# An expert-choice encoder layer on one core: the third expert matrix loaded as pairs of neighbouring rows

## The chip, the core and the metric

The kernel runs on one core of a Trainium2 chip. The metric is the device time of one execution in microseconds (us); the number that counts is the median of the runs shown. TensorE (PE) multiplies matrices, VectorE (DVE) and ScalarE (ACT) work element by element, GpSimd (POOL) does small side work, and SyncE (SP) issues the transfers, which 16 DMA engines carry from device memory (HBM) to the on-chip buffer.

## What is computed

One layer of a hybrid encoder for 512 tokens of 1024 features: three token mixers, an output projection and a norm, and then a mixture of 16 experts of which each picks its 64 best tokens. The change lies in the experts:

```python
def expert_choice_ffn(x, router_w, w_gate, w_up, w_down):
    aff = softmax(einsum('bsd,de->bse', x, router_w))
    gate, idx = top_k(swapaxes(aff, 1, 2), cap)              # cap = 64 tokens an expert
    xs = x[idx]
    h = silu(einsum('becd,edf->becf', xs, w_gate)) * einsum('becd,edf->becf', xs, w_up)
    y = einsum('becf,efd->becd', h, w_down) * gate[..., None]
    # y of all experts is added to the rows of the tokens
```

An expert has three fp32 weights of 8 MB: `w_gate` and `w_up` of 1024 x 2048 (rows of 8 KB) and `w_down` of 2048 x 1024 (rows of 4 KB). 16 experts have 403 MB of them.

## The kernel before

The token mixers, the output projection and the router take the first part of the execution. Then come the experts, one after the other. The weights of expert e are loaded in 24 transfers of 1 MB each, named in the trace e0g, e0u, e0d for its gate, up and down weights (eight loads k = 0 to 7 of each), into tiles of 128 partitions x 2048 floats. `seq` (lines 798 to 811) lists all 384 loads in order, `load_experts` issues them through `load` (line 63) from SP's queue, in that order. A tile is a slot of a shared pool, so a load may start when the tile that had its slot has been read; in the rows of the profile such a wait of SP names the PE work that reads it. The loads run ahead of the arithmetic as far as the slots go. Expert 0's loads are issued while the router still works.

PE takes the loads in the same order. For each gate or up load `ff_mm` (line 1203) multiplies the expert's gathered tokens with it (tiles `pgt` and `pup`). The 2048 hidden features lie as 128 partitions x 1024 columns in `hb`: partitions 0 to 63 hold features 0 to 1023 of the 64 tokens, partitions 64 to 127 hold features 1024 to 2047. ScalarE applies SiLU, VectorE multiplies by the up product (line 1364), then eight transposes on PE (line 1368, tile `pht`) turn `hb` into `hT`, 128 columns at a time. ScalarE copies the first four of them out, VectorE the last four (line 1370). In a transpose the piece of `hb` is the stationary operand (it goes through a weight load, PEld in the profile), and the identity matrix is streamed past it.

`down` (line 1212) multiplies `hT` with the eight down loads (tile `py`). Load k holds, on partition p, row k*128 + p of the weight for the first 1024 features and row 1024 + k*128 + p for the second: two pieces of 4 KB per partition. So load k goes with column block k of `hT`, its first half of slots and its second. The last expert's down weight has a layout and a function of its own (`last_down`). Pairs of experts are gathered together, and the results are added to the rows of the tokens with one-hot products (`pxg`, `pcb`, `pst`), which PE does between the loads of other experts.

Of the kernel before, what the change touches and what calls it, by code (L numbers as in the profile page):

```python
# [7 lines left out]
I32 = mybir.dt.int32  # L8
# [20 lines left out]
def tile_hybrid_layer(ctx, tc, pk, w2p, xT, x, wlv, wa, wak, wmb, wout, eg, eu, ed, out):  # L29
# [45 lines left out]
    # ------------------------------------------------------------ first loads  # L75
# [15 lines left out]
    # the tensor engine's clock and the activation table are up before the first loads arrive  # L91
# [14 lines left out]
    # ------------------------------------------------------------ constants  # L106
# [5 lines left out]
    apT = at_t[:, 0:1536].rearrange("p (b g n) -> p b g n", b=2, g=2)     # transposed probabilities, two buffers  # L112
    dm = at_t[:, 1536:1920]
    masks = at_t[:, 0:384].bitcast(I32).rearrange("p (a b) -> p a b", a=6)    # of the levels, before that
    gD = at_t[:, 384:896].rearrange("p (h b t) -> p h b t", h=2, b=4)         # pairs in 64 tokens
# [16 lines left out]
    # ------------------------------------------------------------ GLA low rank, GLA v, attention v  # L132
    misc = S("misc", [128, 4, 512])          # low rank part, attention v, second key tile's decays
    av = misc[:, 1, :].rearrange("p (a b) -> p a b", a=4)
    # the low rank part is stacked three times on the partitions: high, low, high with high, high, low of its weights
# [8 lines left out]
    def b_mm(pb, k):  # L144
        """products of k-tile k, those first whose parts are there first"""
        for part in range(3):
            for (tb, c), p in pb.items():
                a = (xl if part == 1 else xh)[k // 4][:, k % 4, tb * 128:(tb + 1) * 128]
                w = (wl if part == 2 else wh)[k // 3][:, k % 3, c * 336:(c + 1) * 336]
                PE.matmul(p[:, :336], a, w, start=k == 0 and part == 0, stop=k == 7 and part == 2)  # L150
# [20 lines left out]
    # ------------------------------------------------------------ weight stream of the [feature, token] blocks  # L171
    # block names in order; pairs share a load
    names = ["gq0", "gq1", "gk0", "gk1", "gr0", "gr1", "gr2", "gr3", "ak", "aq0", "aq1", "aq2", "aq3",
             "ch0", "cc0", "cb0", "ch1", "cc1", "cb1", "ch2", "cc2", "cb2", "ch3", "cc3", "cb3"]
    units = []                                   # (kind, chunk, index in chunk)
# [84 lines left out]
    # ------------------------------------------------------------ GLA  # L260
    gqk = S("gqk", [128, 2, 2, 512])             # [q|k, tile, t]
    adec = {}                                    # (direction, tile) -> decay [128, 512]
# [57 lines left out]
    class Gla:  # L320
        """one pass over the two heads of key tile i"""
# [22 lines left out]
        def prep(self, m):  # L344
            """factors of level m (blocks of 2m tokens, decays to the middle)"""
# [59 lines left out]
        def post(self, m):  # L405
            if m >= 256:
                # the rows of k and the state of each half of the tokens
                t = H("gkt" if m == 256 else "gst")
                if m == 256:
                    self.kt = t  # L410
                    A.copy(t, self.p)
                else:
                    self.state = t
                    A.copy(t[:, 0:256], self.p[:, 0:256])
                return
# [70 lines left out]
    def rsqrt(r, h, t):  # L486
        """r = (4.5 h) ** -0.5, as a list of steps: a guess of 1.5 times that from the exponent bits with the sign
        turned, a Newton step that turns it as well and a step of third order that takes the 1.5 away"""
# [9 lines left out]
    def weave(a, b):  # L498
        """the steps of two lists in turn, so that neither waits for its own last step"""
        for i in range(max(len(a), len(b))):  # L500
            run(a[i:i + 1] + b[i:i + 1])
# [5 lines left out]
    # ------------------------------------------------------------ attention  # L507
    aq = [S(f"aq{i}", [128, 4, 512], F32R) for i in range(2)]     # high and low parts
# [10 lines left out]
    class Att:  # L519
        """heads j and j + 4, query block b"""  # L520
# [79 lines left out]
    # ------------------------------------------------------------ short convolution  # L600
# [25 lines left out]
    # ------------------------------------------------------------ side work beside the blocks  # L626
# [3 lines left out]
    class Step:  # L630
        """work beside a segment of the blocks: before it, on the tensor engine after it, and afterwards"""
# [38 lines left out]
    def overlay(a, b, at):  # L670
        """steps b beside steps a from position at of a"""
        for i, o in enumerate(b):
            if at + i < len(a):
                a[at + i].join(o)
            else:
                a.append(o)
        return a
# [79 lines left out]
    # ------------------------------------------------------------ gates, branches, merge  # L757
    order = ("g", "c", "a")
    accs, mh, ml = [], [], []
    # ------------------------------------------------------------ output projection: its weights  # L760
# [36 lines left out]
    # ------------------------------------------------------------ expert weights  # L797
    seq = []
    for e in range(NE):
# [4 lines left out]
        for k in range(8):  # L804
            if e < NE - 1:
                seq.append((ed[e].rearrange("(h q p) d -> q p h d", h=2, p=128)[k], e, "d", k))
            else:
                src = ed[e].rearrange("(f p) d -> p f d", p=128)
                seq.append((src[:, k % 2 * 8:k % 2 * 8 + 8, k // 2 * 256:k // 2 * 256 + 256], e, "d", k))
    # the spare buffers take a load each: y's an early one, h's the last one before the experts begin  # L810
# [5 lines left out]
    def load_experts(upto, after):  # L816
        while nload[0] < min(upto, len(seq)):
# [7 lines left out]
            if kind == "d":  # L825
# [7 lines left out]
            chunk[e, kind, k] = t  # L833
# [46 lines left out]
    # ------------------------------------------------------------ output projection, first norm, router  # L880
# [6 lines left out]
    hbt = X("hbt", [128, 2048])                   # transposed rows, then one load of the experts, then h both ways  # L887
# [10 lines left out]
    Sg = X("Sg", [128, 4, 2, 64])                 # before the one-hot matrices, what the router needs  # L898
# [28 lines left out]
    def aggr(tb, n):  # L927
        """means and variances of the rows of n token blocks, as a list of steps"""
        return [lambda i=i: V.bn_aggr(mvs[:, i, :], stat[:, i]) for i in range(tb, tb + n)]

    def stats(tb, n):
        """reciprocal deviations of the rows of n token blocks, as a list of steps"""
# [5 lines left out]
    def route_t(tb, half):  # L938
        """transposed rows of token block tb, half of the columns"""
# [6 lines left out]
    def route_m(tb, half):  # L946
        """router products of token block tb, half of the columns"""
# [8 lines left out]
    def keep(n):  # L956
        """products without a use, so that the tensor engine's clock stays up where it would wait"""
# [4 lines left out]
    def rows(tb):  # L962
        """normalized rows before scale and shift, in place"""
# [4 lines left out]
    def centered(tb, n):  # L968
        """the negated logits of n token blocks before the rows' deviations and the shift, as a list of steps"""
# [3 lines left out]
    def soft(tb, n):  # L973
        """exponentials of the logits of n token blocks, and their sums"""
# [20 lines left out]
    def top64(dst, src):  # L995
        """the 64 largest values of each row in order, eight a round, as a list of steps"""
# [8 lines left out]
    # the slots of all parts of the weights are held before the experts' loads may take the others  # L1005
# [85 lines left out]
    def bcast(i, half, dg, scale=1.0, E=V, after=None):  # L1091
        """half of vector i of the norms' scales and shifts on all partitions"""
# [13 lines left out]
    # ------------------------------------------------------------ top tokens of each expert  # L1106
# [27 lines left out]
    # ------------------------------------------------------------ experts  # L1134

    def one_hot(i):
        """[token, slot] of the pair of experts 2i, 2i+1"""
# [4 lines left out]
    def gates(i):  # L1142
        """affinities of the chosen tokens by slot, for both halves of the partitions"""
# [8 lines left out]
    def gather(i, d):  # L1152
        """d-tile of the gathered tokens of pair i"""
# [7 lines left out]
    def st_pair():  # L1161
        """[slot, token] of the pair of experts in Sg, in both orders"""
# [9 lines left out]
    def st_last():  # L1172
        """[slot, token] of the last expert, twice"""
# [12 lines left out]
    def to_acc(half, tb):  # L1186
        """alpha times the normed rows"""
# [23 lines left out]
    def down(p, e, k):  # L1211
        w = chunk[e, "d", k]
        for half in range(2):
            for g in range(2):
                dh = g ^ (e % 2)
                PE.matmul(p[g * 64:(g + 1) * 64, :], hT[:, k, half * 64:(half + 1) * 64],  # L1216
                          w[:, half, dh * 512:(dh + 1) * 512], start=k == 0 and half == 0,
                          stop=k == 7 and half == 1)
# [17 lines left out]
    def last_down(k):  # L1236
        """the last expert's output by blocks of 256 columns of two loads each"""
# [10 lines left out]
        if 2 <= k < 6:  # L1248
            # the last block of the rows themselves, to which its products are added
# [12 lines left out]
    def last_combine(b):  # L1262
        """a block added to the rows"""
# [17 lines left out]
    def row(tb, c):  # L1281
        """columns c of a block of rows, the last ones of which are not in acc"""
# [7 lines left out]
    for e in range(NE):  # L1290
        for kind in "gud":
# [65 lines left out]
            if kind == "g":  # L1357
                for c in range(2):
                    A.activation(hb[:, c * 512:(c + 1) * 512], pg[c], AF.Silu)  # L1359
                if e == LAST:  # L1360
                    A.activation(rts[:, 0:1], one[:, 0:1], AF.Sqrt)      # its table is loaded early
            elif kind == "u":
                for c in range(2):
                    V.tensor_mul(hb[:, c * 512:(c + 1) * 512], pu[c], hb[:, c * 512:(c + 1) * 512])  # L1364
                for c in range(2):
                    p = P("pht")
                    for i in range(4):
                        PE.transpose(p[:, i * 128:(i + 1) * 128], hb[:, c * 512 + i * 128:c * 512 + i * 128 + 128],  # L1368
                                     ident)
# [34 lines left out]
    # reciprocal square roots: a Newton step after the root of the activation table  # L1404
# [92 lines left out]
```

## Time and profile before

| what | us or share |
|---|---|
| median of 3 runs (1485.08 to 1487.37) | 1485.46 |
| span of the profiled execution, first to last instruction | 1485.3 |
| PE busy | 93% |
| VectorE, ScalarE busy | 30%, 19% |
| bytes moved, mean rate | 449.32 MB, 303 GB/s |

The profiled execution's span stands 0.2 us under the median of the runs, and inside of their spread. The busy shares are means over stages that differ: the mixers take about the first 450 us, the router runs until about 535 us, the experts' arithmetic follows until about 1465 us, and the last norm and the stores end it. The rate of the transfers in the experts' stage is far above the mean.

### The profile page before, as it was taken

What the parts mean: (1) busy time and instruction counts of PE and PEld (TensorE: products, weight loads), DVE (VectorE), ACT (ScalarE), POOL (GpSimd) and SP (SyncE); (2) the same over time, 40 slices, a digit from 0 to 9 for tenths busy, and PEclk for the clock granted to TensorE, in tenths of its full rate; (3) what the DMA queues carried; (4) which work ended last, traced back from release to release, by engine and by line L of the source; (5) the groups of instructions that cost most, each with busy time, mean ns of one, the idle gap of its engine ahead of it and who ended that gap; (6) DMA issues with size and microseconds to landing.
All of it is one profiled execution on the core that took longest, in us unless ns stands there. A gap on an engine that the chain in (4) does not pass through costs nothing.

```text
span 1485.3 us, 17870 instructions
## 1 busy us (share of the span) xinstructions
PE 1380.5 (93%) x7458; PEld 770.7 (52%) x7458; DVE 447.0 (30%) x903; ACT 288.3 (19%) x546; POOL 88.9 (6%) x127
## 2 busy tenths in 40 slices
PE   9988999999999989999999889989979989998995
PEld 8765777888888855533434423422523433332343
DVE  5569586423344533112021011002011011000236
ACT  4623455222234120101001000100100100000011
POOL 0267200000000010000000000000000000000001
PEclk9999999999999999999999999999999999999998
DMA  6110121232338689999999999999999999999995
GB/s 224 44 58 34 53 69 60 85 107 85 107 129 339 276 338 383 398 415 421 414 417 419 414 421 415 415 420 415 419 416 415 421 414 418 418 415 420 415 384 169
DMA packets 89631, 449.32 MB, mean 303 GB/s; under 512 B 7280, under 2 KB 15600, under 8 KB 55248
## 3 DMA queue, kind: packets, MB, share of 16 engines
q1 hardware_dynamic: 89552, 448.20, 75.5%
q8 instruction: 58, 0.95, 0.3%
q14 instruction: 21, 0.17, 0.0%
HBM read 446.07 MB, written 2.10 MB: 302 GB/s over the span
## 4 chain that ended last, share of the span: by engine, by line
PE 65%; DMA 27%; DVE 6%; issue 1%; ACT 0%; POOL 0%; SPq 0%; DVEq 0%; POOLq 0%; ACTq 0%
PE pgt L1208 10%; PE pup L1208 10%; PE py L1216 5%; PE pxg L1156 5%; PE pm L858 3%; PE pm L860 3%; PE pm L859 3%; PE pa L248 3%; PE pa L250 2%; PE pa L249 2%; PE pb L150 2%; PE pbr L868 1%; PE pbr L867 1%; PE pbr L866 1%; DMA e5d<-in_ed_dram 1%; DMA e14g<-in_eg_dram 1%
## 5 line engine op out<-in xcount | busy, mean ns | idle before, releaser
L1201 DVE TENSOR_TENSOR acc<-acc,pcb 128x512 f32<-128x512 f32 x64 | 41.1, 684 | 221.5 <-PE pcb L1199 221.5
L1225 DVE SCALAR_TENSOR_TENSOR yl<-py,small,late 64x512 fp32r<-64x512 f32 x30 | 22.5, 749 | 246.3 <-ACT late L1224 246.3
L1156 PEld LDWEIGHTS pxg<-Sg,xres 128*128 128x128 f32 x512 | 61.9, 191 | 50.6 <-issue 43.0
L248 PE MATMUL pa<-xh,wb 128*128 128x512 f32 x200 | 84.0, 420 | 0.0
L249 PE MATMUL pa<-xl,wb 128*128 128x512 f32 x200 | 79.8, 399 | 0.0
L250 PE MATMUL pa<-xh,wb 128*128 128x512 f32 x200 | 79.7, 399 | 0.0
L858 PE MATMUL pm<-xh,wmh 128*128 128x512 f32 x192 | 74.8, 390 | 0.0
L859 PE MATMUL pm<-xl,wmh 128*128 128x512 f32 x192 | 74.7, 389 | 0.0
L860 PE MATMUL pm<-xh,wml 128*128 128x512 f32 x192 | 74.7, 389 | 0.0
L1156 PE MATMUL pxg<-Sg,xres 128*128 128x128 f32 x512 | 73.8, 287 | 0.1
L1224 ACT ACTIVATE late<-py,small 64x512 fp32r<-64x512 f32 x30 | 20.5, 682 | 265.8 <-PE py L1216 253.7
L1370 ACT COPY hbt<-pht 128x512 f32<-128x512 f32 x16 | 9.4, 585 | 250.1 <-PE pht L1368 250.1
L1364 DVE TENSOR_TENSOR hbt<-pup,hbt 128x512 f32<-128x512 f32 x32 | 22.1, 692 | 112.2 <-PE pup L1208 112.2
L1150 DVE COPY small<-pgt 128x2 f32<-128x2 f32 x8 | 1.3, 159 | 172.1 <-PE pgt L1148 172.1
L1380 POOL TENSOR_SCALAR small<-small 128x1 f32<-128x1 f32 x1 | 0.2, 227 | 878.0 <-DVE small L1377 878.0
L248 PEld LDWEIGHTS pa<-xh,wb 128*128 128x128 f32 x200 | 38.1, 190 | 11.5 <-issue 2.9
L1359 ACT ACTIVATE hbt<-pgt 128x512 f32<-128x512 f32 x32 | 19.0, 597 | 127.9 <-PE pgt L1208 127.9
L208 DVE TENSOR_TENSOR wml<-wmr,wmh 128x1536 fp32r<-128x1536 f32 x24 | 42.1, 1752 | 4.1 <-ACT wmh L205 4.1
L250 PEld LDWEIGHTS pa<-xh,wb 128*128 128x128 f32 x200 | 38.5, 192 | 8.7
L249 PEld LDWEIGHTS pa<-xl,wb 128*128 128x128 f32 x200 | 38.3, 192 | 6.7
L858 PEld LDWEIGHTS pm<-xh,wmh 128*128 128x128 f32 x192 | 36.0, 188 | 7.7 <-issue 0.2
L859 PEld LDWEIGHTS pm<-xl,wmh 128*128 128x128 f32 x192 | 36.0, 188 | 7.5
(413 smaller groups left out, 2411.3 us busy)
## 6 DMA issues: line engine op xcount, KB each, us to landing
wmr<-in_wmb_dram SPq DMA_DIRECT2D x24, 768.0 KB, 4.2
wr<-in_wa_dram SPq DMA_DIRECT2D x12, 1024.0 KB, 4.8
e0d<-in_ed_dram SPq DMA_DIRECT2D x8, 1024.0 KB, 10.7
e1g<-in_eg_dram SPq DMA_DIRECT2D x8, 1024.0 KB, 4.8
e1u<-in_eu_dram SPq DMA_DIRECT2D x8, 1024.0 KB, 7.2
e1d<-in_ed_dram SPq DMA_DIRECT2D x8, 1024.0 KB, 7.9
e2g<-in_eg_dram SPq DMA_DIRECT2D x8, 1024.0 KB, 6.3
e2u<-in_eu_dram SPq DMA_DIRECT2D x8, 1024.0 KB, 10.4
```

Source lines behind the costliest of these rows:

```text
L150: PE.matmul(p[:, :336], a, w, start=k == 0 and part == 0, stop=k == 7 and part == 2)
L208: sp2[u] = V.tensor_sub(l, raw2[u], f32(h))
L248: PE.matmul(p, w[:, 0, k, :], XH(k), start=k == 0, stop=False)
L249: PE.matmul(p, w[:, 0, k, :], XL(k), start=False, stop=False)
L250: PE.matmul(p, w[:, 1, k, :], XH(k), start=False, stop=k == 7)
L858: PE.matmul(p, h[:, k, :], XH(k), start=k == 0, stop=False)
L859: PE.matmul(p, h[:, k, :], XL(k), start=False, stop=False)
L860: PE.matmul(p, l[:, k, :], XH(k), start=False, stop=k == 7)
L1156: PE.matmul(p[:, 0:128], xr_(tb)[:, d * 128:(d + 1) * 128], Sg[:, tb].rearrange("p a b -> p (a b)"), start=tb == 0, stop=tb == 3)
L1201: V.tensor_add(r, r, p)
L1208: PE.matmul(p[c][g * 64:(g + 1) * 64, :], l, w[:, g * 1024 + c * 512:g * 1024 + c * 512 + 512], start=k == 0, stop=k == 7)
L1216: PE.matmul(p[g * 64:(g + 1) * 64, :], hT[:, k, half * 64:(half + 1) * 64], w[:, half, dh * 512:(dh + 1) * 512], start=k == 0 and half == ...
```

## The change

The down weights of experts 0 to 14 are cut into loads in another way. Load k now holds rows 256k to 256k + 255; partition p gets rows 256k + 2p and 256k + 2p + 1, which lie side by side in HBM, so that each partition's part is one piece of 8 KB instead of two of 4 KB. Loads 0 to 3 hold the first 1024 features, loads 4 to 7 the others. Since a load's rows on 128 partitions are now every second row, a transpose reads every second column of `hb`: even columns of a block of 256 for one column block of `hT`, odd ones for the next. `down` takes the blocks of `hT` in the new order: load k uses blocks 2(k mod 4) and 2(k mod 4) + 1, of one half of the slots. The last expert stays as it was. Comments that the diff also removes are left out here.

```diff
@@ load list
             if e < NE - 1:
-                seq.append((ed[e].rearrange("(h q p) d -> q p h d", h=2, p=128)[k], e, "d", k))
+                seq.append((ed[e].rearrange("(k p r) d -> k p (r d)", p=128, r=2)[k], e, "d", k))
...
@@ load_experts
-            if kind == "d":
+            if len(src.shape) == 3:
                 t = t.rearrange("p (a b) -> p a b", a=src.shape[1])
...
-            chunk[e, kind, k] = t
+            chunk[e, kind, k] = t if kind != "d" or len(src.shape) == 3 else t.rearrange("p (a b) -> p a b", a=2)
...
@@ down
-        for half in range(2):
+        half = k // 4
+        for r in range(2):
             for g in range(2):
                 dh = g ^ (e % 2)
-                PE.matmul(p[g * 64:(g + 1) * 64, :], hT[:, k, half * 64:(half + 1) * 64],
-                          w[:, half, dh * 512:(dh + 1) * 512], start=k == 0 and half == 0,
-                          stop=k == 7 and half == 1)
+                PE.matmul(p[g * 64:(g + 1) * 64, :], hT[:, k % 4 * 2 + r, half * 64:(half + 1) * 64],
+                          w[:, r, dh * 512:(dh + 1) * 512], start=k == 0 and r == 0,
+                          stop=k == 7 and r == 1)
...
@@ experts
                     for i in range(4):
-                        PE.transpose(p[:, i * 128:(i + 1) * 128], hb[:, c * 512 + i * 128:c * 512 + i * 128 + 128],
-                                     ident)
+                        c0, step = (c * 512 + i // 2 * 256 + i % 2, 2) if e < LAST else (c * 512 + i * 128, 1)
+                        PE.transpose(p[:, i * 128:(i + 1) * 128], hb[:, c0:c0 + 127 * step + 1:step], ident)
```

The order of the instructions stays as it is; what an instruction reads changes. SP's queue before, around expert 2's down loads (a row is a load: its tile, the weight it comes from, and the shape of the tile):

```order
L63 DMA e2u7_4443<-in_eu_dram 128x2048
L63 DMA e2d0_4445<-in_ed_dram 128x2x1024
L63 DMA e2d1_4447<-in_ed_dram 128x2x1024
...
L63 DMA e2d7_4459<-in_ed_dram 128x2x1024
L63 DMA e3g0_4461<-in_eg_dram 128x2048
```

And the same place now:

```order
L63 DMA e2u7_4443<-in_eu_dram 128x2048
L63 DMA e2d0_4445<-in_ed_dram 128x2048
L63 DMA e2d1_4447<-in_ed_dram 128x2048
...
L63 DMA e2d7_4459<-in_ed_dram 128x2048
L63 DMA e3g0_4461<-in_eg_dram 128x2048
```

No load has moved; the down loads now have the shape of the gate and up loads around them. PE before, from the end of expert 14's up products to the first of expert 15 (`pht` are the transposes, `py` the down products):

```order
L1208 MATMUL pup1_7626<-e14u7_5019,xgb_5157 64x512 x2
L1368 MATMUL pht_7709<-ident_118,hbt_3718 128x128 x4
L1368 MATMUL pht_7715<-ident_118,hbt_3718 128x128 x4
L1216 MATMUL py_7721<-e14d0_5021,hbt_3718 64x512 x4
...
L1216 MATMUL py_7721<-e14d7_5035,hbt_3718 64x512 x4
L1208 MATMUL pgt0_7762<-e15g0_5037,xgb_5157 64x512 x2
```

And now:

```order
L1208 MATMUL pup1_7626<-e14u7_5019,xgb_5157 64x512 x2
L1372 MATMUL pht_7709<-ident_118,hbt_3718 128x128 x4
L1372 MATMUL pht_7715<-ident_118,hbt_3718 128x128 x4
L1218 MATMUL py_7721<-e14d0_5021,hbt_3718 64x512 x4
...
L1218 MATMUL py_7721<-e14d7_5035,hbt_3718 64x512 x4
L1208 MATMUL pgt0_7762<-e15g0_5037,xgb_5157 64x512 x2
```

The counts and the order are the same; only the line numbers differ, and which columns of `hb` and which blocks of `hT` are read, which such rows don't show.

## Rows read from the trace of the kernel before

**Rows 1.** The page: the span in 40 slices.

```profile
PE   9988999999999989999999889989979989998995
...
PEclk9999999999999999999999999999999999999998
DMA  6110121232338689999999999999999999999995
GB/s 224 44 58 34 53 69 60 85 107 85 107 129 339 276 338 383 398 415 421 414 417 419 414 421 415 415 420 415 419 416 415 421 414 418 418 415 420 415 384 169
```

**Rows 2.** The chain that ended last, in order of time: start us, us, what.

```profile
677.71 13.88 PE py L1216 x64
...
821.37 1.22 PE pup L1208 x5
822.59 20.92 DMA e5d<-in_ed_dram
...
1383.57 18.22 DMA e15g<-in_eg_dram
1401.83 1.94 PE pgt L1208 x8
...
1443.18 0.70 DVE hbt L1364
1444.02 0.63 PE pht L1368 x4
1444.65 5.33 PE py L1244 x48
```

**Rows 3.** DMA issues: tile, queue, count, KB each, median us to landing.

```profile
e1d<-in_ed_dram SPq DMA_DIRECT2D x8, 1024.0 KB, 7.9
e2g<-in_eg_dram SPq DMA_DIRECT2D x8, 1024.0 KB, 6.3
e2u<-in_eu_dram SPq DMA_DIRECT2D x8, 1024.0 KB, 10.4
e2d<-in_ed_dram SPq DMA_DIRECT2D x8, 1024.0 KB, 17.2
e3g<-in_eg_dram SPq DMA_DIRECT2D x8, 1024.0 KB, 19.9
...
e14d<-in_ed_dram SPq DMA_DIRECT2D x8, 1024.0 KB, 20.0
```

**Rows 4.** Tile e8d: its issues, first and last start us, and landing.

```profile
L63 SPq DMA_DIRECT2D e8d<-in_ed_dram x8: 368/963/4670, 997.1 to 1016.8; - x8
...
DMA to landing us min/median/max: 18.1/20.0/20.3
```

**Rows 5.** Busy time by stretch, the last two columns DMA share and GB/s.

```profile
540.00:600.00 60.00, 59.71 (x328) 30.17 (x327) 15.09 (x26) 7.98 (x14) 0.67 (x3) 1.00 0.97 379
616.00:648.00 32.00, 31.80 (x152) 13.58 (x150) 4.47 (x9) 1.95 (x3) 0.00 (x0) 1.00 1.00 409
771.00:790.00 19.00, 18.79 (x86) 7.00 (x84) 5.93 (x9) 0.58 (x1) 0.00 (x0) 1.00 1.03 410
1012.00:1032.00 20.00, 18.62 (x83) 6.42 (x80) 4.64 (x7) 0.59 (x1) 0.00 (x0) 1.00 1.03 410
1040.00:1070.00 30.00, 30.00 (x186) 15.58 (x188) 0.94 (x5) 4.86 (x10) 0.00 (x0) 1.00 1.01 421
1280.00:1310.00 30.00, 29.45 (x182) 14.52 (x183) 2.55 (x7) 5.59 (x12) 0.00 (x0) 1.00 1.01 421
1372.00:1397.00 25.00, 23.27 (x103) 8.21 (x104) 7.61 (x15) 0.58 (x1) 0.00 (x0) 1.00 1.02 412
```

**Rows 6.** Products of three gate tiles: duration min/median/max, first and last start us.

```profile
L1208 PE MATMUL pgt<-e0g,xga x56: 592/592/644, 535.2 to 554.3; 128*64 128x512 f32 x56
...
L1208 PE MATMUL pgt<-e5g,xga x64: 592/592/643, 796.0 to 816.7; 128*64 128x512 f32 x64
...
L1208 PE MATMUL pgt<-e15g,xgb x64: 592/592/643, 1401.8 to 1421.0; 128*64 128x512 f32 x64
```

**Rows 7.** Tile pht, the transposes: duration ns min/median/max, first and last start us.

```profile
L1368 PEld LDWEIGHTS pht<-ident,hbt x128: 137/141/145, 570.3 to 1444.3; 128*128 128x128 f32 x128
L1368 PE MATMUL pht<-ident,hbt x128: 272/273/332, 570.3 to 1444.4; 128*128 128x128 f32 x128
```

**Rows 8.** Timeline at expert 8's transposes: start us, us, what, count, idle before.

```profile
1019.28 0.42 PEld L1368 LDWEIGHTS pht<-ident,hbt 128*128 128x128 f32 x4 [0.44 <-DVE hbt L1364]
...
1019.87 1.51 PE L1216 MATMUL py<-e8d,hbt 128*64 128x512 f32 x6
1019.98 0.69 DVE L1370 COPY hbt<-pht 128x512 f32<-128x512 f32 x1 [0.75 <-PE pht L1368]
```

**Rows 9.** PE's waits from 822 to 1402 us: total us, times, longest.

```profile
PE py L1216 <- DMA e13d<-in_ed_dram: 4.5, 6, 1.4
...
PE py L1216 <- DMA e8d<-in_ed_dram: 2.1, 4, 0.6
```

## Prediction

> **What bounds the kernel now.** I read the slices of the span first [rows 1]. PE is busy at 80 to 90% and more almost everywhere, at full clock, and from about a third of the span on the 16 DMA engines are as busy. A share of busy time doesn't say which of two full engines sets the end, so I read the chain of waits next [rows 2]. Up to 822 us the chain of the experts runs on PE alone. From 822 us (a load of e5d) it is made of transfers with stretches of PE between them, and the last transfer in it is e15g's first load, which ends at 1401.8 us. From there to the end (83.5 us) it holds no transfer: expert 15's products, the norm, the stores. So the end is the landing of e15g's first load plus 83.5 us, and the question is when that load lands.
>
> For this I read how long a load takes from issue to landing [rows 3]. e2g's take 6.3 us, e2u's 10.4, e2d's 17.2, and from e3g on it stays at 19.9 to 20, which is eight loads of about 2.5 us: the queue in front of the DMA engines fills up during expert 2 and never empties before expert 15. From e2d on, a load thus begins when the one ahead of it is done, whatever PE does. Before that the engines are not full: share 0.97 and 379 GB/s from 540 to 600 us, where e1's loads move [rows 5].
>
> Then PE's own pace [rows 6]. Expert 0's gate products begin at 535.2 us and expert 5's at 796.0: 52.2 us an expert while PE waits for no load. From there to expert 15 at 1401.8 it is 60.6 us an expert. PE has about 8.4 us an expert to spare; the loads set the pace.
>
> Last, the rate of the loads, in stretches that hold one kind. Such a stretch is found from the issues: e8d's loads are issued from 997.1 to 1016.8 us and land about 20 us later, so they move from about 1012 to 1035 us [rows 4]. In three such stretches of down loads the engines moved 410, 410 and 412 GB/s (771, 1012 and 1372 us); in two stretches of gate and up loads, of pieces of 8 KB, 421 and 421 (1040 and 1280 us). The DMA share is 1.01 to 1.03 in all five: the engines are full in both, and get less through with pieces of 4 KB [rows 5].
>
> **The change, part by part.** *The loads.* A load is 1024 KB, 1.0486 million bytes: 2.557 us at 410 GB/s and 2.491 us at 421. I take 410, since the third stretch touches 8 KB pieces at its edges (the engines are not in step there). The new down loads have the shape of the gate and up loads, so I give them their 2.491 us: 0.067 us less for each. (Per engine a load is 16 pieces of 160 ns before, 8 of 311 ns after: a piece saved is worth 8 ns.) Of the 15 x 8 changed loads those count that lie in the full queue and ahead of e15g's first: e2d to e14d, 13 x 8 = 104. 104 x 0.067 = **6.9 us**. e0d and e1d move while the engines have gaps, where a shorter load only makes a longer gap; I give them nothing (were e1d to count too, 0.5 us). The rates are shown to a whole GB/s: 409.5 against 421.5 with e1d's eight is 112 x 0.073 = 8.2 us, and 412.5 against 420.5 on 104 loads is 5.0 us. Those are the bounds of this term.
>
> The Trainium skill ("DMA: Bandwidth & Descriptors", section "Why small descriptors are slow (HBM only)") gives a fixed overhead of about 3 cycles per packet and 32 bytes of metadata per operation; at the 850 MHz and 32 bytes a cycle of its section on the 436 GB/s that is an estimate of 4.7 ns a piece, not 8 ns, and the sum by it would be 3.9 us. I keep the 6.9 us of the rows.
>
> *The transposes.* Their weight load now reads every second column. No row of before shows a weight load with a stride. Today it takes 141 ns and lies beside a product of 273 ns; four products end within 0.7 us [rows 7, 8]. From below it costs nothing. From above I double it (it passes over twice the bytes): 8 x 0.141 = 1.1 us an expert on PE if nothing hides it. In experts 5 to 14 PE's waits of 2.1 to 4.5 us for the down loads right behind hide this [rows 9]; in experts 2 to 4 PE has no such wait, but there the queue is full and the end is not set by PE. What is left is experts 0 and 1, whose later reads free slots later while the engines still have gaps: 0 to 2.3 us. I take 0, since a doubled load would still be about as short as the product beside it.
>
> The skill ("SBUF — State Buffer", its note on cachelines) has lines of 16 bytes in the buffer, read at full rate if two accesses in a row fall in one line; a stride of two floats does that, so by it the cost is nothing. No run here has shown it yet.
>
> *The order of reading `hT`.* Load 2 now needs the second half of `hT`, which load 4 needed before. VectorE's copy of that half begins 0.11 us after the first down product at 1019.87 us and lasts 0.69: done at 1020.67 us [rows 8]. Eight loads' products take 13.88 us [rows 2], 1.73 a load, so load 2 begins at 1023.3 us, 2.7 us after the copy. Cost nothing, with that cover. The number and order of loads, products, copies and slots stay.
>
> The sum: 1485.3 - 6.9 = 1478.4 us for the span. The median of the runs stands 0.2 us above the profiled span, so **1478.6 us**. After it the loads take 24 x 2.491 = 59.8 us an expert against PE's 52.2: they still set the pace, and no new bound is met.
>
> **The rivals.** *No change: the down stretches are slow for a reason other than the size of the pieces*, say where those weights lie in HBM, or what the chip does beside them. For it: from 616 to 648 us, where gate and up loads of 8 KB move, the rate is 409 GB/s as well [rows 5]. Against it: the queue was only filling up there [rows 3], the share is 1.00 and not 1.01 to 1.03, and the difference between the kinds comes back in each of the later stretches, with PE waiting and with PE full. It gives 1485.5 us; chance 0.08. The Trainium skill's DMA page ("Specifications") speaks for this one, as it has line rate from 512 bytes on; 410 against 421 GB/s doesn't agree with that to the last 2.6%, if the size is the cause.
>
> *Part of it.* The pieces get cheaper by less than the stretches promise, or experts 0 and 1 pay for their strided reads, or the queue fills up one expert later (8 loads fewer): some half of the term, 3.5 us, 1482.0 us; chance 0.07.
>
> *Slower: the strided weight load is so slow that PE becomes the bound.* The loads need (1401.8 - 535.2) / 15 = 57.8 us an expert on average over all 15, PE 52.2. From 5.6 us more on PE an expert, 0.7 us a transpose (273 ns to about 0.97 us, each one in full on the path), PE sets the end. If a transpose took 1.3 us, an expert would take 60.4 us, and the time would be 535.2 + 15 x 60.4 + 83.5 + 0.2 = 1525 us. For it: no row shows this read. Against it: it needs 3.5 times the duration of a whole transpose, of which the weight load is the half that lies beside the product. Chance 0.05.
>
> **How the numbers follow.** The forecast has 0.80. A measurement of this kernel can't tell less than about 0.2%, 3.0 us, from no change. The forecast and most of the partial case lie beyond that: faster 0.87. No change holds 0.08, slower 0.05. The range goes from 1476.0 us (the largest saving, 8.2 us, and 1.3 us for the scatter of runs, which is 2.3 us wide before) to 1482.3 us (the smallest, 5.0 us, and the partial case up to its 3.5 us).
>
> **What the profile of the changed kernel would show.** Right: the down stretches move 420 GB/s or more, like the gate and up stretches; some 15 thousand fewer packets; the pace of experts 5 to 15 near 60.0 us; e15g's first products near 1395 us and the tail behind them still 83.5 us; PE in expert 0 to 4 at the same 52.2 us, and the transposes at 273 ns. Wrong in the loads: down stretches at 410 with half the packets. Wrong in the transposes: a longer `pht` with a later first down product, and PE's waits for down loads gone. Wrong in the place: a gap in the DMA share behind 615 us, where slots come free too late for the faster loads, or a longer stretch behind e15g.

## The result, and the profile after

The changed kernel takes 1478.79 us in the median of four runs (1477.96 to 1478.91), the kernel before 1486.3 (1485.08 to 1487.37, four runs). The ratio is 0.9948, with a 95% interval from 0.9934 to 0.9962: about 7.5 us or 0.5% faster. The forecast was 1478.6 us, in a range of 1476.0 to 1482.3.

The profiled execution has a span of 1476.8 us. From its page, the packets, and the same slices as [rows 1]:

```profile
PE   9987999999999989999999989989989989998995
...
PEclk9999999999999989999999999999999999999998
DMA  6111121232338689999999999999999999999995
GB/s 225 44 58 41 46 75 55 86 107 86 107 121 336 278 332 386 387 423 421 422 420 422 420 422 422 420 422 421 421 421 422 422 421 421 421 420 421 422 385 169
DMA packets 74271, 449.32 MB, mean 304 GB/s; under 512 B 7280, under 2 KB 15600, under 8 KB 24528
```

The busy digits are nearly the same. What has changed is the rate: before, the slices of the experts' stage went up and down between 414 and 421 GB/s, now they stand at 420 to 423. There are 74271 packets where the page of before counts 89631: 15360 fewer, which is one for each partition of each of the 120 changed loads.

Stretches that hold down loads alone, found by their issues as with [rows 4], and one with e9's gate and up loads (they answer to [rows 5]; the last two columns are the DMA share and GB/s):

```profile
771.00:789.00 18.00, 17.88 (x80) 7.08 (x80) 5.93 (x9) 0.59 (x1) 0.00 (x0) 1.00 1.01 421
1011.00:1029.00 18.00, 16.78 (x78) 5.93 (x76) 3.36 (x5) 0.59 (x1) 0.00 (x0) 1.00 1.01 421
1372.00:1390.00 18.00, 16.77 (x76) 5.85 (x76) 4.16 (x9) 0.59 (x1) 0.00 (x0) 1.00 1.01 422
1034.00:1066.00 32.00, 31.46 (x192) 16.31 (x192) 1.81 (x6) 5.01 (x11) 0.00 (x0) 1.00 1.01 421
```

Down loads now move like gate and up loads. Where the time went out is seen in the first and last start of the gate products, as in [rows 6]:

```profile
L1208 PE MATMUL pgt<-e0g,xga x56: 592/592/644, 534.4 to 553.5; 128*64 128x512 f32 x56
...
L1208 PE MATMUL pgt<-e5g,xga x64: 592/592/644, 795.6 to 816.4; 128*64 128x512 f32 x64
...
L1208 PE MATMUL pgt<-e15g,xgb x64: 592/592/643, 1393.4 to 1412.5; 128*64 128x512 f32 x64
```

From expert 0 to expert 5 it is 52.2 us an expert, as before, while PE waits for no load. From 5 to 15 it is 59.8 instead of 60.6. From expert 0 to 15 the stretch is 859.0 us instead of 866.6, and behind e15g's first products 83.4 us are left, as before. The two spans differ by 8.5 us: 7.6 of it lies in this stretch and 0.8 ahead of expert 0, where nothing was changed (spans of the kernel before itself range over some 3 us, from 1483.0 to 1486.4). So the stretch between the first products of expert 0 and of expert 15 is the better measure, and the experiments below are read by it.

The chain still runs through e15g's first load (it answers to [rows 2]):

```profile
1353.65 19.79 DMA e14d<-in_ed_dram
1373.50 19.84 DMA e15g<-in_eg_dram
1393.38 1.94 PE pgt L1208 x8
```

A down load now takes the 19.8 us from issue to landing that a gate load takes. The tile of the transposes, as [rows 7], holds a surprise:

```profile
L1372 PEld LDWEIGHTS pht<-ident,hbt x128: 138/209/219, 569.5 to 1435.8; 128*128 128x128 f32 x128
L1372 PE MATMUL pht<-ident,hbt x128: 272/283/389, 569.5 to 1435.9; 128*128 128x128 f32 x128
```

A weight load that reads every second column takes 209 ns in the median, 140 where it doesn't (the last expert's); before, all were near 141. The products beside it went from 273 to 283 ns.

### The profile page after: what moved, and what is told of

Its sections match the earlier page's. It is cut to its first block, busy times and chain, and to the rows that moved or that the text cites. A ratio compares the mean times of both kernels' runs of the same rounds, so it can differ in the third digit from the quotient of the medians.

```text
span 1476.8 us, 17870 instructions
## 1 busy us (share of the span) xinstructions
PE 1378.8 (93%) x7458; PEld 771.0 (52%) x7458; DVE 447.0 (30%) x903; ACT 288.5 (20%) x546; POOL 88.9 (6%) x127
## 2 busy tenths in 40 slices
DMA packets 74271, 449.32 MB, mean 304 GB/s; under 512 B 7280, under 2 KB 15600, under 8 KB 24528
## 4 chain that ended last, share of the span: by engine, by line
PE 49%; DMA 44%; DVE 6%; issue 1%; ACT 0%; POOL 0%; SPq 0%; DVEq 0%; POOLq 0%; ACTq 0%
PE pgt L1208 5%; PE pup L1208 5%; PE py L1218 4%; PE pm L858 3%; PE pm L860 3%; PE pm L859 3%; PE pa L248 3%; PE pa L249 2%; PE pa L250 2%; PE pb L150 2%; PE pxg L1156 2%; PE pbr L868 1%; PE pbr L866 1%; PE pbr L867 1%; DMA e9u<-in_eu_dram 1%; DMA e13u<-in_eu_dram 1%
## 5 line engine op out<-in xcount | busy, mean ns | idle before, releaser
L860 PEld LDWEIGHTS pm<-xh,wml 128*128 128x128 f32 x192 | 36.0, 188 | 7.5
```

What stands on the lines that cost most here:

```text
L860: PE.matmul(p, l[:, k, :], XH(k), start=False, stop=k == 7)
```

## The experiments

Three theories could explain the gain. *Size*: an engine pays for each piece beside its bytes, and half the pieces are gone. *Place*: a load now comes from one block of 1 MB of HBM and no longer from two halves 4 MB apart. *PE*: the new order of the products or the strided transposes changed something there. The starts below are the first gate products of experts 0 and 15 in each profile, one profile for each kernel.

| kernel | expert 0 | expert 15 | stretch, us | ratio of times (95%) |
|---|---|---|---|---|
| before | 535.2 | 1401.8 | 866.6 | 1 |
| changed | 534.4 | 1393.4 | 859.0 | 0.9948 (0.9934 to 0.9962) |
| 4 KB pieces from one block | 534.1 | 1400.8 | 866.7 | 1.0000 (0.9991 to 1.0008) |
| strided transposes alone | 533.8 | 1400.6 | 866.8 | 1.0003 (0.9994 to 1.0012) |
| 2 KB pieces | 534.4 | 1415.8 | 881.4 | 1.0106 (1.0093 to 1.012) |
| 8 KB pieces, plain columns | 533.4 | 1392.1 | 858.7 | 0.9948 (0.9933 to 0.9963) |
| change in experts 0 and 1 alone | 534.9 | 1401.2 | 866.3 | one run |
| change in experts 8 to 14 alone | 533.5 | 1395.8 | 862.3 | 0.9974 (0.9964 to 0.9984) |
| changed, 16 more products an expert | 533.8 | 1392.6 | 858.8 | 0.9956 (0.9939 to 0.9972) |
| changed, 33 more products an expert | 535.2 | 1416.1 | 880.9 | 1.0094 (1.0079 to 1.011) |

**4 KB pieces from one block.** Against the changed kernel:

```diff
-                seq.append((ed[e].rearrange("(k p r) d -> k p (r d)", p=128, r=2)[k], e, "d", k))
+                seq.append((ed[e].rearrange("(k r p) d -> k p r d", p=128, r=2)[k], e, "d", k))
...
-                        c0, step = (c * 512 + i // 2 * 256 + i % 2, 2) if e < LAST else (c * 512 + i * 128, 1)
-                        PE.transpose(p[:, i * 128:(i + 1) * 128], hb[:, c0:c0 + 127 * step + 1:step], ident)
+                        PE.transpose(p[:, i * 128:(i + 1) * 128], hb[:, c * 512 + i * 128:c * 512 + i * 128 + 128],
+                                     ident)
```

> Each down load of experts 0 to 14 still comes from one block of 1 MB and down takes the blocks of hT in the new order, but a partition gets rows 256k + p and 256k + 128 + p, two pieces of 4 KB, and the transposes read neighbouring columns. If the size of the pieces is the cause: the time of the kernel before (ratio 1.000, no more than 0.001 off), down stretches near 410 GB/s, 60.6 us an expert from expert 5 to 15. If the place is the cause (one block of 1 MB instead of two halves 4 MB apart), or the new order of the products: the time of the changed kernel, ratio 0.995, 421 GB/s, 60.0 us an expert or less.

The time is that of the kernel before. Its stretches, e8d's loads first and then e9's gate and up loads:

```profile
1011.00:1031.00 20.00, 18.54 (x82) 6.33 (x80) 4.64 (x7) 0.58 (x1) 0.00 (x0) 1.00 1.02 409
1039.00:1069.00 30.00, 30.00 (x186) 15.59 (x184) 0.86 (x5) 4.85 (x10) 0.00 (x0) 1.00 1.01 421
```

The block of 1 MB and the new order of the products are there, the pieces are of 4 KB, and the whole gain is gone. The place is out as a cause, and the new order of the products with it.

**Strided transposes alone.** Against the kernel before (its transposes are those of the changed kernel):

```diff
-                seq.append((ed[e].rearrange("(h q p) d -> q p h d", h=2, p=128)[k], e, "d", k))
+                seq.append((ed[e].rearrange("(h q p r) d -> q r p h d", h=2, p=128, r=2)[k // 2, k % 2], e, "d", k))
```

> The strided transposes alone: pieces of 4 KB, one from each half of the features as before, old order of the products, but a load holds every second row, so that the transposes read every second column. If the size of the pieces is the cause and the strided read is hidden: ratio 1.000. If the strided read or the spread of the rows in HBM costs something in the end: above 1.001. If the transposes brought the gain: 0.995. The weight loads of the transposes should take the 209 ns of the changed kernel, not 141.

It takes the time of before, with the slower weight loads:

```profile
L1370 PEld LDWEIGHTS pht<-ident,hbt x128: 138/209/219, 569.0 to 1443.1; 128*128 128x128 f32 x128
L1370 PE MATMUL pht<-ident,hbt x128: 272/283/388, 569.0 to 1443.2; 128*128 128x128 f32 x128
```

So the stride brings no gain and costs nothing that the time shows, though a weight load takes half as long again. The last four transposes of expert 2, as a step of the chain that ended last, take 0.75 us in the changed kernel and 0.66 before: 0.09 us on PE, which can show only where PE sets the pace.

**2 KB pieces.** Against the kernel before, with `w[:, dh, half, :]` in `down`:

```diff
-                seq.append((ed[e].rearrange("(h q p) d -> q p h d", h=2, p=128)[k], e, "d", k))
+                seq.append((ed[e].rearrange("(h q p) (c d) -> q p c h d", h=2, p=128, c=2)[k], e, "d", k))
```

> The kernel before with its down loads cut into four pieces of 2 KB per partition instead of two of 4 KB; transposes, order and rows as before. If each piece costs an engine about 8 ns more than its bytes: 16 more pieces an engine in each load, 0.13 us a load, 104 loads: 14 us more, ratio 1.009, down stretches near 390 GB/s. If pieces of 2 KB move at the same rate as those of 4 KB and another thing made the changed kernel faster: ratio 1.000.

The ratio is 1.0106, 15 us slower, and the stretch is 14.8 us longer where 14 were expected. A stretch of e8d's loads, and one of e9's gate and up loads in the same run:

```profile
1024.00:1041.00 17.00, 14.13 (x66) 4.46 (x64) 2.02 (x3) 0.59 (x1) 0.00 (x0) 1.00 1.05 390
...
1046.00:1076.00 30.00, 29.45 (x183) 14.73 (x181) 1.94 (x7) 5.53 (x11) 0.00 (x0) 1.00 1.01 421
```

390 GB/s with 2 KB, 410 with 4 KB, 421 with 8 KB, and 421 beside each of them for the loads that weren't touched. 16 pieces more on each engine for each of 104 loads cost 14.8 us: 8.9 ns a piece. 8 fewer in the changed kernel gave 7.6 us: 9.1 ns a piece. The two agree.

One thing more goes with the pieces: SP's issuing of the loads. For e8d's eight loads, first in the changed kernel and then with 2 KB (min/median/max in ns; before, [rows 4], it was 368/963/4670):

```profile
L63 SPq DMA_DIRECT2D e8d<-in_ed_dram x8: 327/328/328, 992.7 to 1010.1; - x8
DMA to landing us min/median/max: 19.8/19.8/19.8
...
L63 SPq DMA_DIRECT2D e8d<-in_ed_dram x8: 612/2522/8281, 1003.4 to 1028.2; - x8
DMA to landing us min/median/max: 14.4/15.7/20.6
```

So smaller pieces are slower to issue as well, and fewer loads are queued ahead. That is not what costs the time: even with 2 KB a load is issued 14.4 us or more before it lands, the time of some five loads, and the DMA share is 1.05, so the engines always have work. The records of the single packets in the kept traces show the cost itself: in the experts' stage a packet takes 314 ns on average with 8 KB, 164 with 4 KB and 89 with 2 KB. Two packets for one cost about 13 ns of packet time; shares above 1 mean that packets of an engine overlap a little, so that 9 of the 13 reach the time.

**8 KB pieces, plain columns.** The changed kernel with the transposes of before.

```diff
-                        c0, step = (c * 512 + i // 2 * 256 + i % 2, 2) if e < LAST else (c * 512 + i * 128, 1)
+                        c0, step = c * 512 + i * 128, 1
```

> The changed kernel with transposes that read neighbouring columns, as before; the products then pair rows of the weight with other hidden features (that part of the computation is changed). If the strided read lies wholly beside other work: the time of the changed kernel, ratio 0.995, with weight loads of 141 ns in the transposes instead of 209. If it costs something in the end: down to 1 us an expert, ratio 0.985 to 0.994.

The ratio is the same 0.9948, the weight loads are back at 141 ns in its trace, and the stretch is 858.7 us, 0.3 less than with the stride, hardly more than the 0.2 us by which three kernels with 4 KB pieces differ. The strided read lies beside other work but for some 0.3 us in all, if that.

**The change in some experts alone.** The condition `e < NE - 1` of the new loads, `e < LAST` of the strided columns, and the new order in `down` are replaced by one of

```diff
+            if e < 2:
...
+            if 8 <= e < NE - 1:
```

> The change in experts 0 and 1 alone; 2 to 14 load pieces of 4 KB as before. From the first gate products of expert 0 to those of expert 15 the kernel before needs 866.6 us and the changed one 859.0. If loads that move before the queue is full count nothing: 866.6 us. If e1's count: 866.0. If all 16 count: 865.4. (The time of a run can't tell these apart, the stretch in the trace can: three kernels with pieces of 4 KB gave 866.6, 866.7 and 866.8.)

> The change in experts 8 to 14 alone, 56 loads behind the full queue, after the first waits of PE for loads. If each load behind the full queue counts alike, 7.6 us over 104 loads: 4.1 us less, 862.5 us from expert 0 to 15, ratio 0.997. If the gain needed the loads of the early experts, where PE is the chain (a longer lead that is used up later): near 866.6 us, ratio 0.999 to 1.000.

The gate products of experts 0 and 15, of the first kernel and then of the second:

```profile
L1210 PE MATMUL pgt<-e0g,xga x56: 592/592/644, 534.9 to 554.0; 128*64 128x512 f32 x56
...
L1210 PE MATMUL pgt<-e15g,xgb x64: 592/592/643, 1401.2 to 1420.4; 128*64 128x512 f32 x64
```

```profile
L1210 PE MATMUL pgt<-e0g,xga x56: 592/592/644, 533.5 to 552.6; 128*64 128x512 f32 x56
...
L1210 PE MATMUL pgt<-e15g,xgb x64: 592/592/643, 1395.8 to 1414.9; 128*64 128x512 f32 x64
```

16 loads of experts 0 and 1 are worth 0.3 us (866.3 against 866.6), where 16 behind the full queue are worth 1.2. They count for next to nothing; whether a few of e1's count can't be told, since three kernels with 4 KB pieces differ by 0.2 us among themselves. The 56 loads of experts 8 to 14 give 4.3 us (4.1 expected), the ratio 0.9974 agrees, and a lead from the early experts is not needed for it.

**More work on PE.** In the changed kernel, behind the eight transposes (`keep` makes products whose result nothing reads):

```diff
+                if 2 <= e < LAST:
+                    keep(16)
```

and 33 instead of 16 in the second kernel.

> The changed kernel with 16 products without a use behind the transposes of experts 2 to 14, 0.24 us each: 3.8 us more on PE an expert. If the loads set the pace up to 5.6 us more on PE: the time of the changed kernel, ratio 0.995, stretch from expert 0 to 15 of 859 us. If PE sets it: 13 x 3.8 = 50 us more, ratio 1.028; if PE sets it up to the first wait for a load (experts 2 to 4): 11 us more, ratio 1.002.

> The same with 33 products: 7.9 us more on PE an expert, 60.1 us without any wait for a load. The stretch from expert 2 to 15 is then 13 x 60.1 = 781 us if PE sets it, instead of 753 us: 28 us more than the changed kernel, ratio 1.014. If the loads still hide it: ratio 0.995.

With 16 products the stretch stays at 858.8 us: all of it is hidden. It is there in the early experts, where it takes 272.0 us from expert 0 to expert 5 instead of 261.2 (3.6 us more in each of experts 2 to 4), and is made up for by expert 15:

```profile
L1208 PE MATMUL pgt<-e0g,xga x56: 592/592/644, 533.8 to 552.9; 128*64 128x512 f32 x56
...
L1208 PE MATMUL pgt<-e5g,xga x64: 592/592/644, 805.8 to 826.6; 128*64 128x512 f32 x64
...
L1208 PE MATMUL pgt<-e15g,xgb x64: 592/592/643, 1392.6 to 1411.7; 128*64 128x512 f32 x64
```

With 33 products the stretch grows by 21.9 us, and the view of PE's waits names no wait for a load between 640 and 1412 us: PE sets the pace now.

```profile
L1208 PE MATMUL pgt<-e0g,xga x56: 592/592/644, 535.2 to 554.3; 128*64 128x512 f32 x56
...
L1208 PE MATMUL pgt<-e5g,xga x64: 592/592/644, 818.6 to 839.4; 128*64 128x512 f32 x64
...
L1208 PE MATMUL pgt<-e15g,xgb x64: 592/592/644, 1416.1 to 1435.2; 128*64 128x512 f32 x64
```

28 us were expected. From expert 0 to expert 5 it takes 283.4 us, 22.2 more than in the changed kernel, so the products cost 7.4 us in each of experts 2 to 4 instead of 7.9: over 13 experts that is the 6 us by which the expectation was too high. Of 13 x 7.4 = 96 us, 22 show, so about 74 us were there to hide in, 5.7 us for each of the 13 experts.

## Why the prediction was right

**What sets the end: shown.** The end is e15g's first landing plus a tail that the loads don't touch (83.5 us before, 83.4 after), and that landing comes at the pace of the loads from expert 2 on. Extra work on PE of 3.6 us an expert costs nothing; at 7.4 us PE takes over.

**The cause: shown.** It is the number of pieces. Taking the block and the order without the size brings nothing, the stride alone brings nothing, smaller pieces cost by the same rule, and the gain goes with the number of changed loads behind the full queue. Not separated is the cut from the jump: in every kernel with more pieces the next piece of a partition also lies elsewhere in HBM (512 KB or 4 MB on, with no difference between the two), and neighbouring rows cut into two pieces were not tried.

**The size of the term: somewhat small.** I took 0.067 us a load from 410 against 421 GB/s, 6.9 us in all; it measured 7.6 us, 0.073 a load, or 9 ns a piece instead of 8. It lies inside of the bounds of 5.0 to 8.2. Rounding is enough to account for it (409.5 against 421.5 GB/s, which the prediction takes for its upper bound, is 0.073 us a load); that it was this is not shown. The stretch over 13 experts needs no rate.

**The base: too low, and luck in the total.** The sum takes the profiled span of 1485.3 us and adds 0.2, which is to start from the median of the three runs, 1485.46. With a fourth run that median became 1486.3, and the kernel before, run again beside the experiments, had medians of 1486.05 (11 runs) and 1486.75 (21). To set that span 0.2 us under that median was a mistake as well, as if the two were of one execution: the later runs list both numbers, and the time of a run is mostly about 2.0 us above its own span (1478.77 and 1476.8 for the changed kernel), while runs of the kernel before with a span of 1485.3 took 1487.2 to 1487.6. That mistake cancels out of the sum; the low median doesn't. Taken from 1486.3, the sum would have been 1479.4; the measured 1478.8 lies 0.6 under that. The 1478.6 came nearer by luck: a base 0.8 us too low and a saving some 0.7 us too small go against each other.

**The strided read: cost right, reason wrong in part.** I took nothing on the path, with up to 141 ns a transpose as the upper bound. The weight load did get slower, by 68 ns, about half of the bound, and the products went to 283 ns where the prediction named 273 as a sign of being right. The note on cachelines in the Trainium skill ("SBUF — State Buffer") would have it free at a stride of two floats; 209 against 141 ns doesn't agree for this read. It is the cover that kept it out of the time: with the product beside it only 0.09 us an expert is left on PE, and behind the full queue the loads hide that, as they hide the 3.6 us of the 16 products.

**The new order of `hT`: right.** The first half and the second are copied as before, and the kernel with that order and 4 KB pieces has the time of before.

**Where it counts: right.** Experts 0 and 1 gave 0.3 us for 16 loads, at the edge of what the trace can tell.

**The rivals.** *No change* is refuted, and with it the place in HBM. The 409 GB/s from 616 to 648 us that spoke for it is still there in the changed kernel, whose gate and up loads are the same. The Trainium skill ("DMA: Bandwidth & Descriptors", "Specifications") has line rate from 512 bytes on; 390, 410 and 421 GB/s don't agree with that. The estimate of 4.7 ns a piece, from the Trainium skill ("DMA: Bandwidth & Descriptors", "Why small descriptors are slow (HBM only)"), is about half of the measured 9. *Part of it* is out too: the term came whole. *Slower by PE* didn't happen, but its point was about right: its sum with the changed kernel's stretch, 859.0 / 15 - 52.2, gives 5.1 us an expert to spare (5.6 was for the loads of before), and the 74 us that hid behind the loads are 5.0 for each of 15. The strided reads, at some 0.3 us in all, were far from it.

## What to carry to other kernels

Where the queue of loads never empties, the sum of (pieces x fixed cost + bytes / rate) sets the pace of the stage: here 9 ns a piece on each engine, 2.6% between 4 KB and 8 KB. Rows that a matrix product contracts over may be dealt to the partitions in any order, as long as the other operand is read in the same one; so neighbouring rows on one partition make pieces twice as long for free, if the stride that it puts on the other operand has cover. Before you set a profiled span against a median, look whether they are of one execution, and what lies around the span: the 2 us there are a quarter of such a gain.

## What was not expected of the hardware

A weight load of 128 x 128 floats with a stride of two floats took 209 ns (219 at most) and 141 without a stride. The changed kernel, the two with more work on PE and the one with the strided transposes alone show the 209; the kernel before and the kernels with 4 KB pieces from one block, with 2 KB pieces and with plain columns are at 141. Nothing here tried another stride or another type.

With all pieces of one size the pace of the experts is even but for single steps: from expert 9 to 10 it took 61.2 us (gate products from 1032.5 and 1093.7 us), from 10 to 11 59.7. Another such step came four experts later, from 13 to 14. In the view of SP's waits the longest wait for a landing is 3.4 us among e9u's loads and 3.3 among e13u's, and 2.1 for most other tiles: one load lands late in each. Why was not tried.

Pieces above 8 KB were not tried either: a row of the gate and up weights is 8 KB, and a slot holds no more per partition.
